# Changing the order of the first projections, the buffers of the RG-LRU stage and the share of projections beside it, in a one-core S5 and RG-LRU layer

## The chip, the core and the metric

The kernel runs on one core of one Trainium2 chip. The metric is the device time of one execution in microseconds; less is better. Three runs of the kernel before gave a median of 1853.79 us (1853.48 to 1860.08).

## What is computed

One layer of a diffusion backbone on x (2048 tokens, 1024 channels) behind a context of 256 tokens, all in f32. Both are normalised and modulated, projected to 4096 columns, run through two recurrent branches, gated, projected back and added to x.

```python
z = (rmsnorm(h, norm_g) * (1.0 + sc) + sh) @ w_in            # the same for the context
u_s5, g_s5, u_lru, g_lru = split(z)                          # 1024 columns each
# S5: 64 groups of 64 complex states, both directions, the context first
h_re, h_im = scan(abar, bbar @ u_s5);  y = gelu(c @ h + d * u_s5);  y = y * sigmoid(y @ w_glu + b_glu)
# RG-LRU: tokens in column-major order, both directions d
xc = depthwise_conv4(u_lru)
r, gi = sigmoid(xc @ w_a[d] + b_a[d]), sigmoid(xc @ w_x[d] + b_x[d])    # 16 heads of 64
a = exp(-8 * r * softplus(-lam));  h = scan(a, sqrt(1 - a * a) * gi * xc)
out = rmsnorm(x + gt * (concat(y_s5 * silu(g_s5), y_lru * silu(g_lru)) @ w_out), final_g)
```

## The kernel before, in words

Channels lie on the 128 partitions and tokens along a row. A **block** is 128 of the 1024 channels of one kind (`u_lru`, `g_lru`, `u_s5`, `g_s5`), so each kind has eight. A matmul in near-f32 is three matmuls on a high and a low part (`mm3`, lines 248 to 250), and weights are split into these parts by a cast on ScalarE (L240) and a subtraction on VectorE (L241).

`projections(half, kinds)` goes through the blocks of one half of the tokens. A block has a tile of 512 tokens for each of two quarters and, in the first half for `u` kinds, one of 256 context tokens ("c"). A **step** is one `yield` of it: the three matmuls of one of eight contraction parts, so eight steps make a tile. `merge(main, [side, rate])` advances a side generator by `rate` for each step of the main one; `islice(proj, n)` takes n steps. What is issued in which order is settled when the kernel is built: Tile's scheduler starts from the order of the program, and each engine then works strictly through its own list. Inside the RG-LRU loop TensorE's list is the program's own order (`manual_schedule`).

*First half.* `projections(0, ...)` runs with `prepare()` beside it at 0.1375: the S5 tables on VectorE (`s5_tables`, L625 to 627, with transposes L657 and lag matmuls L673 on TensorE), then the normalisation of quarters 2 and 3 (`xhat`) and the gate row. A `u_lru` tile is copied to `uc` (L314); when the block is complete, `conv` makes the four-tap convolution in `xcv` (L376 on ScalarE, three L379 on VectorE) and stores it to `XC` in DRAM (L381, POOL's queue), the context part first. `uc` and `xcv` have one buffer each.

*RG-LRU stage.* `lru()` handles eight blocks of both directions over 2304 tokens. For each direction five gate steps (L422: four 64x64 matmul tiles for `rr` and `gi`, into one buffer each of the PSUM pools `psG` and `psT`, which have two) are followed by sigmoids (L426). Then tanh (L467), `gi*xc` (L470), exp (L474), sqrt (L482), and `finish`: (a+1)*t (L432), L433, the scans (L437, L439), the sum of directions (L442), the product with the gate `GL` (L446) and the store `YL`. `finish` of a block runs as `prev` beside the gates of the next. The numbers that `lru` yields say how many projection steps of the second half TensorE does there: one behind each gate step, then 8, 8, 8 and 10: 44 for a block.

*S5 stage.* `s5_inputs` (L743, copies L746 to 750) fills `z0` and then `z1`, 32 groups each; `s5_scan` is 144 steps of three small VectorE instructions (L771 to 773) for each; `s5_outputs` (L804, L806) reads a finished scan. The rest of the projections, `out_lru` (matmuls `po`) and the scans are merged by rates. `glu` and `tail`, on TensorE alone, end the kernel.

Of the kernel before, what the change touches and what calls it, by code (L numbers as in the profile page):

```python
# [19 lines left out]
L = 2048  # L20
LC = 256
# [4 lines left out]
T = 16  # L26
# [14 lines left out]
def drain(gen):  # L41
    if gen is not None:
        for _ in gen:
            pass


class Block:
# [204 lines left out]
    def projections(self, half, kinds):  # L252
# [29 lines left out]
        both = [2 * half, 2 * half + 1]  # L282
        blocks = []
# [6 lines left out]
        if half == 0:  # L290
            blocks.remove(("g_lru", 0, both))
            blocks[:1] = [("u_lru", 0, ["c", 0]), ("g_lru", 0, [0]), ("u_lru", 0, [1]), ("g_lru", 0, [1])]
        raw, nxt = self.first if half == 0 else (load(0), None)
# [91 lines left out]
    def lru(self, lp, le):  # L385
# [16 lines left out]

        def load(b):

            xs = big("xs", 1, le)
            for e in range(2):
                o = b * P + 64 - e * 64
                nc.sync.dma_start(out=xs[e * 64:e * 64 + 64, :], in_=self.XC[o:o + 64, :])
            xc = big("xc", 1, le)
            nc.sync.dma_start(out=xc, in_=self.XC[rows(b), :])  # L410
            return xc, xs

# [16 lines left out]
        def finish(b, aa, gi, tt):  # L429

            for d in range(2):
                v.scalar_tensor_tensor(out=tt[d], in0=aa[d], scalar=1.0, in1=tt[d], op0=ALU.add, op1=ALU.mult)  # L432
                v.tensor_mul(out=gi[d], in0=gi[d], in1=tt[d])  # L433
                yield
                f = (lambda t, s: t[:, s]) if d == 0 else (lambda t, s: t[:, s][:, ::-1])
                init = tt[d][:, LC - 1:LC] if d == 0 else tt[d][:, 0:1]
                v.tensor_tensor_scan(out=f(tt[d], c_), data0=f(aa[d], c_), data1=f(gi[d], c_), initial=0.0,  # L437
                                     op0=ALU.mult, op1=ALU.add)
                v.tensor_tensor_scan(out=f(tt[d], x_), data0=f(aa[d], x_), data1=f(gi[d], x_), initial=init,  # L439
                                     op0=ALU.mult, op1=ALU.add)  # L440
                yield
            v.tensor_add(out=tt[1][:, x_], in0=tt[1][:, x_], in1=tt[0][:, x_])  # L442
            yo = big("rr", 3)[:, :L].rearrange("p (j q r) -> p j q r", j=T, q=4)
            g = big("gi", 3)[:, :L]
            nc.sync.dma_start(out=g, in_=self.GL[rows(b), :])
            v.tensor_mul(out=yo, in0=tt[1][:, x_].rearrange("p (q j r) -> p j q r", q=4, j=T),  # L446
                         in1=g.rearrange("p (q j r) -> p j q r", q=4, j=T))
# [4 lines left out]
        xcs = load(0)  # L452
        yield 28
        prev = iter(())
        for b in range(8):
            rr, gi, tt = [], [], []
            for d in range(2):
                rr.append(big("rr", 3))
                gi.append(big("gi", 3))
                for i, _ in enumerate(gates(b, d, gw, xcs, rr[d], gi[d])):  # L460
                    if i % 2 == 0:
                        next(prev, None)
                    yield 1
            drain(prev)
            for d in range(2):
                tt.append(big("tt", 3))
                th = nc.scalar.activation(out=tt[d], in_=rr[d], func=AF.Tanh,  # L467
                                          scale=self.c8h[:, d * 8 + b:d * 8 + b + 1])
            for d in range(2):
                v.tensor_mul(out=gi[d], in0=gi[d], in1=xcs[0])  # L470
            yield 8
            with self.tc.issue_after(th.ins):
# [567 lines left out]
    def build(self):  # L1040
        tc, nc = self.tc, self.nc
        with ExitStack() as es:
# [23 lines left out]
            with ExitStack() as eP:  # L1066
# [13 lines left out]
                with ExitStack() as eA, ExitStack() as eS:  # L1080
# [133 lines left out]
```

## Time and profile before

| | before |
|---|---|
| median of three runs | 1853.79 us |
| profiled execution, its own time | 1854.51 us |
| span of its trace | 1852.7 us |
| PE, DVE, ACT busy | 93%, 63%, 47% of the span |
| first projection matmul, first gate matmul | 54.7, 618.3 us |
| last gate matmul, first copy to `z0` | 943.9, 993.5 us |
| S5 scans, from step 2 to the last | 1061.7 to 1337.8 us |

The span goes from the first to the last instruction; the other 1.8 us lie around it. A busy PE is not PE at its peak, since overlapping matmuls are modelled. PE is TensorE, DVE VectorE, ACT ScalarE, POOL GpSimd; "<-" behind idle time names what ended it.

### The profile page before, as it was taken

What the parts mean: (1) busy time and instruction counts of PE and PEld (TensorE: products, weight loads), DVE (VectorE), ACT (ScalarE), POOL (GpSimd) and SP (SyncE); (2) the same over time, 40 slices, a digit from 0 to 9 for tenths busy, and PEclk for the clock granted to TensorE, in tenths of its full rate; (3) what the DMA queues carried; (4) which work ended last, traced back from release to release, by engine and by line L of the source; (5) the groups of instructions that cost most, each with busy time, mean ns of one, the idle gap of its engine ahead of it and who ended that gap; (6) DMA issues with size and microseconds to landing.
All of it is one profiled execution on the core that took longest, in us unless ns stands there. A gap on an engine that the chain in (4) does not pass through costs nothing.

```text
span 1852.7 us, 25971 instructions
## 1 busy us (share of the span) xinstructions
PE 1714.9 (93%) x9785; PEld 1372.4 (74%) x9785; DVE 1165.6 (63%) x2006; ACT 875.1 (47%) x1382; POOL 138.4 (7%) x268
## 2 busy tenths in 40 slices
PE   7887899999999899999998987869799999999997
PEld 2675778888887465666667876758698899998886
DVE  5789999974124287887774198999800056446663
ACT  3622332222562587786685877216355443222221
POOL 1112222211000000000000000000000000001111
PEclk9888999999999898999999999979899999999999
DMA  9675578876446555667777777228788766556563
GB/s 273 169 172 214 201 237 253 263 266 234 138 137 223 161 208 184 205 233 203 202 201 234 244 233 233 80 62 258 212 246 259 213 209 201 165 159 216 185 193 88
DMA packets 335470, 373.55 MB, mean 202 GB/s; under 512 B 124029, under 2 KB 274161, under 8 KB 323058
## 3 DMA queue, kind: packets, MB, share of 16 engines
q1 hardware_dynamic: 288304, 243.43, 45.8%
q0 software_dynamic: 20672, 94.91, 13.6%
q10 hardware_dynamic: 26370, 33.57, 5.2%
q8 instruction: 77, 1.26, 0.3%
q14 instruction: 47, 0.39, 0.1%
HBM read 233.49 MB, written 138.35 MB: 201 GB/s over the span
## 4 chain that ended last, share of the span: by engine, by line
PE 51%; issue 17%; DVE 16%; DMA 10%; ACT 4%; SPq 1%; POOL 1%; ACTq 0%; DVEq 0%; POOLq 0%
PE pp L248 7%; PE pp L249 7%; PE pp L250 7%; PE po L250 4%; PE po L248 4%; PE po L249 4%; DVE p L771 4%; PE pgl L250 3%; PE pgl L248 3%; PE pgl L249 3%; DVE z L772 3%; DVE z L773 3%; DMA YT<-y 2%; PE pw L743 2%; PE pg L422 1%
## 5 line engine op out<-in xcount | busy, mean ns | idle before, releaser
L248 PE MATMUL pp<-x,w 128*128 128x512 f32 x1024 | 422.9, 413 | 14.0 <-ACT uc L314 13.5
L250 PE MATMUL pp<-x,w 128*128 128x512 f32 x1024 | 407.3, 398 | 2.6 <-DVE w L241 2.6
L249 PE MATMUL pp<-x,w 128*128 128x512 f32 x1024 | 407.4, 398 | 0.0
L248 PEld LDWEIGHTS pp<-x,w 128*128 128x128 f32 x1024 | 194.9, 190 | 117.0 <-issue 65.6
L250 PEld LDWEIGHTS pp<-x,w 128*128 128x128 f32 x1024 | 195.0, 190 | 45.6 <-DVE w L241 3.4
L249 PEld LDWEIGHTS pp<-x,w 128*128 128x128 f32 x1024 | 195.5, 191 | 37.2 <-DVE x L213 1.0
L241 DVE TENSOR_TENSOR w<-wraw,w 128x1024 fp32r<-128x1024 f32 x66 | 80.5, 1220 | 163.0 <-ACT w L240 163.0
L240 ACT CAST w<-wraw 128x1024 fp32r<-128x1024 f32 x66 | 69.1, 1047 | 134.6 <-PE pp L250 101.6
L806 PE MATMUL py<-h,et 128*128 128x128 f32 x512 | 83.5, 288 | 33.3 <-ACT h L799 16.8
L250 PE MATMUL po<-x,w 128*128 128x512 f32 x256 | 101.9, 398 | 7.8 <-DVE w L241 7.8
L771 DVE TENSOR_TENSOR p<-z,A 128x128 f32<-128x128 f32 x288 | 104.0, 379 | 5.7
L248 PE MATMUL po<-x,w 128*128 128x512 f32 x256 | 104.4, 408 | 2.2 <-ACT x L836 1.6
L743 PE MATMUL pw<-u,wt 128*128 128x144 f32 x512 | 77.6, 300 | 26.1 <-DMA wt<-WD 18.2
L249 PE MATMUL po<-x,w 128*128 128x512 f32 x256 | 101.1, 395 | 0.2 <-DVE x L837 0.2
L422 PE MATMUL pg<-xc,gw 64*64 64x512 f32 (+1 forms) x320 | 92.2, 595 | 8.5 <-DMA GL<-ust 8.0
L248 PE MATMUL po<-ws,yh 128*128 128x512 f32 x256 | 99.6, 389 | 0.0
L249 PE MATMUL po<-ws,yh 128*128 128x512 f32 x256 | 99.6, 389 | 0.0
L250 PE MATMUL po<-ws,yl 128*128 128x512 f32 x256 | 99.6, 389 | 0.0
L743 PEld LDWEIGHTS pw<-u,wt 128*128 128x128 f32 x512 | 73.2, 200 | 34.4 <-issue 15.4
L806 PEld LDWEIGHTS py<-h,et 128*128 128x128 f32 x512 | 71.5, 202 | 36.0 <-ACT h L799 19.5
L422 PE MATMUL pg<-xs,gw 64*64 64x512 f32 (+1 forms) x320 | 91.0, 594 | 2.7 <-ACT gi L426 2.7
L379 DVE SCALAR_TENSOR_TENSOR xcv<-uc,vcol,xcv 128x256 f32<-128x256 f32 (+2 forms) x72 | 73.0, 1014 | 22.0 <-ACT xcv L376 21.3
(258 smaller groups left out, 3557.0 us busy)
## 6 DMA issues: line engine op xcount, KB each, us to landing
wraw<-in_w_in_dram SPq DMA_DIRECT2D x50, 512.0 KB
WS<-w POOLq DMA_DIRECT2D x24, 1024.0 KB, 7.0
w<-WS SPq DMA_DIRECT2D x24, 1024.0 KB
u<-ZU SPq DMA_DIRECT2D x64, 288.0 KB
ED<-E POOLq DMA_DIRECT2D x16, 1024.0 KB, 5.6
WD<-Wt POOLq DMA_DIRECT2D x32, 512.0 KB, 4.2
wt<-WD SPq DMA_DIRECT2D x32, 512.0 KB
et<-ED SPq DMA_DIRECT2D x32, 512.0 KB
```

The lines of the kernel that those rows point to most:

```text
L240: copy(out=w[:, 0], in_=raw)
L241: self.nc.vector.tensor_sub(out=w[:, 1], in0=raw, in1=w[:, 0])
L248: nc.tensor.matmul(ps, lhsT=whi(k), rhs=xhi(k), start=(k == 0), stop=False)
L249: nc.tensor.matmul(ps, lhsT=whi(k), rhs=xlo(k), start=False, stop=False)
L250: nc.tensor.matmul(ps, lhsT=wlo(k), rhs=xhi(k), start=False, stop=(k == KT - 1))
L379: nc.vector.scalar_tensor_tensor(out=xc, in0=u[:, o + k:o + k + N], scalar=cw[:, k * 8 + b:k * 8 + b + 1], in1=xc, op0=ALU.mult, op1=ALU.add)
L422: nc.tensor.matmul(pss[w][e * 64:e * 64 + 64, :n], lhsT=gw[ws, d, e, :], rhs=xcs[(w + e) % 2][ws, o:o + n], start=True, stop=True, tile_po ...
L743: nc.tensor.matmul(pw[:, c, :], lhsT=w[:, gi, kt, c, :], rhs=u[:, kt, :], start=(kt == 0), stop=(kt == 1))
L771: v.tensor_mul(out=p, in0=cur.unsqueeze(1).to_broadcast([P, 2, 2, 32]), in1=self.A16[:, :, :, gs])
L772: v.tensor_add(out=nxt, in0=nxt, in1=p[:, 0])
L773: v.tensor_add(out=nxt, in0=nxt, in1=p[:, 1, ::-1])
L806: nc.tensor.matmul(o, lhsT=ms(e[:, i, gi]), rhs=h[:, i, :], start=False, stop=(i == 1))
```

## The change

Four things are changed. (1) In the first half `u_lru` and `g_lru` of block 0 stay in front; then come `u_s5`, `g_s5`, `g_lru` and, last, the other seven `u_lru`. (2) In the RG-LRU stage `gi` gets four buffers and `tt` two; the scans write into `gi`, the gate `GL` is loaded into the spent `rr` and the product goes into the spent `gi`, so `rr` and `gi` no longer take extra buffers. The loads of the next block's `xs`, `gw` and `xc` are issued right behind the gates. (3) Gate steps come in pairs, with one projection step behind each pair and 8, 8 and 16 later: 37 for a block instead of 44. (4) Behind the stage 32 projection steps are taken beside `s5_inputs` of `z0` at 1.0 instead of 56 at 0.57, and the rates of the next merge are lower, as more steps are left.

```diff
         if half == 0:
-            blocks.remove(("g_lru", 0, both))
-            blocks[:1] = [("u_lru", 0, ["c", 0]), ("g_lru", 0, [0]), ("u_lru", 0, [1]), ("g_lru", 0, [1])]
+            blocks = [("u_lru", 0, ["c", 0]), ("g_lru", 0, [0]), ("u_lru", 0, [1]), ("g_lru", 0, [1])] + [
+                bl for bl in blocks if bl[:2] not in (("u_lru", 0), ("g_lru", 0))]
...
-                init = tt[d][:, LC - 1:LC] if d == 0 else tt[d][:, 0:1]
-                v.tensor_tensor_scan(out=f(tt[d], c_), data0=f(aa[d], c_), data1=f(gi[d], c_), initial=0.0,
+                init = gi[d][:, LC - 1:LC] if d == 0 else gi[d][:, 0:1]
+                v.tensor_tensor_scan(out=f(gi[d], c_), data0=f(aa[d], c_), data1=f(gi[d], c_), initial=0.0,
...
-            v.tensor_add(out=tt[1][:, x_], in0=tt[1][:, x_], in1=tt[0][:, x_])
-            yo = big("rr", 3)[:, :L].rearrange("p (j q r) -> p j q r", j=T, q=4)
-            g = big("gi", 3)[:, :L]
+            g = aa[1][:, :L]
             nc.sync.dma_start(out=g, in_=self.GL[rows(b), :])
+            v.tensor_add(out=gi[1][:, x_], in0=gi[1][:, x_], in1=gi[0][:, x_])
+            yield
+            yo = gi[0][:, :L].rearrange("p (j q r) -> p j q r", j=T, q=4)
...
                 rr.append(big("rr", 3))
-                gi.append(big("gi", 3))
-                for i, _ in enumerate(gates(b, d, gw, xcs, rr[d], gi[d])):
-                    if i % 2 == 0:
+                gi.append(big("gi", 4))
+                for i, _ in enumerate(gates(b, d, gw, (xc, xs), rr[d], gi[d])):
+                    if (d * 5 + i) % 2 == 1:
+                        yield 1
                         next(prev, None)
-                    yield 1
-            drain(prev)
+                v.tensor_mul(out=gi[d], in0=gi[d], in1=xc)
+            if b < 7:
+                xs, gw, xc = load_xs(b + 1), weights(b + 1), load_xc(b + 1)
             for d in range(2):
-                tt.append(big("tt", 3))
+                tt.append(big("tt", 2))
...
-            if b < 7:
-                gw, xcs = weights(b + 1), load(b + 1)
-            yield 8
...
-            yield 10
+            yield 16
...
-                    merge(self.projections(0, (("u_lru",), ("u_s5",), ("g_lru",), ("g_s5",))), [side, 0.1375])
+                    merge(self.projections(0, (("u_s5",), ("g_s5",), ("g_lru",), ("u_lru",))), [side, 0.1375])
...
-                merge(islice(proj, 56), [sin[0], 0.57])
+                merge(islice(proj, 32), [sin[0], 1.0])
...
-                merge(proj, [sin[1], 0.5], [scans[0], 1.5], [load, 0.17])
+                merge(proj, [sin[1], 0.25], [scans[0], 0.9], [load, 0.1])
```

The built orders show where this lands. On VectorE, in the first half, this stood in a stretch of `u_lru` blocks before; xcv is the convolution, E, W and ot are the S5 tables:

```order
L379 SCALAR_TENSOR_TENSOR xcv<-uc,vcol_372,xcv 128x256
L626 TENSOR_TENSOR ot<-PI,WE 128x512
L379 SCALAR_TENSOR_TENSOR xcv<-uc,vcol_372,xcv 128x256
L627 TENSOR_TENSOR W<-W,ot 128x512
L379 SCALAR_TENSOR_TENSOR xcv<-uc,vcol_372,xcv 128x256
L626 TENSOR_TENSOR ot<-PI,WE 128x512
```

And this stands in the changed kernel where the second `u_lru` block is convolved (line numbers are three higher there from `lru` on):

```order
L630 TENSOR_TENSOR W<-W,ot 128x512
L241 TENSOR_TENSOR w<-wraw,w 128x1024
L688 SCALAR_TENSOR_TENSOR kk<-dmask,dcol,psk 128x16
L690 TENSOR_TENSOR kk<-kk,psk 128x16
L379 SCALAR_TENSOR_TENSOR xcv<-uc,vcol_372,xcv 128x256 x3
L241 TENSOR_TENSOR w<-wraw,w 128x1024
L383 COPY halo<-uc 128x3
L379 SCALAR_TENSOR_TENSOR xcv<-uc,vcol_372,xcv 128x1022 x3
```

All E and W rows now stand ahead of the seven moved convolutions, which are no longer mixed with them.

On TensorE, in the gates of an RG-LRU block before (pg is a gate tile, pp a projection):

```order
L422 MATMUL pg<-xc,gw 64x512
L422 MATMUL pg<-xs,gw 64x512 x2
L422 MATMUL pg<-xc,gw 64x512
L248 MATMUL pp<-x_4498,w 128x512
L249 MATMUL pp<-x_4498,w 128x512
L250 MATMUL pp<-x_4498,w 128x512
```

And now:

```order
L425 MATMUL pg<-xc,gw 64x512
L425 MATMUL pg<-xs,gw 64x512 x2
L425 MATMUL pg<-xc,gw 64x512 x2
L425 MATMUL pg<-xs,gw 64x512 x2
L425 MATMUL pg<-xc,gw 64x512
L248 MATMUL pp<-x_4286,w 128x512
L249 MATMUL pp<-x_4286,w 128x512
L250 MATMUL pp<-x_4286,w 128x512
```

Two gate steps, which fill all four buffers of `psG` and `psT`, now stand together.

On VectorE, where the second S5 scan joins the first before (`z_7430` is the first scan, `z_7431` the second):

```order
L771 TENSOR_TENSOR p<-z_7430,A_318 128x128
L771 TENSOR_TENSOR p<-z_7431,A_318 128x128
L772 TENSOR_TENSOR z_7430<-z_7430,p 128x64
L772 TENSOR_TENSOR z_7431<-z_7431,p 128x64
L773 TENSOR_TENSOR z_7430<-z_7430,p 128x64
L773 TENSOR_TENSOR z_7431<-z_7431,p 128x64
```

And the changed kernel, shortly ahead of that place (`z_7201` is the first scan):

```order
L776 TENSOR_TENSOR z_7201<-z_7201,p 128x64
L774 TENSOR_TENSOR p<-z_7201,A_318 128x128
L241 TENSOR_TENSOR w<-wraw,w 128x1024
L775 TENSOR_TENSOR z_7201<-z_7201,p 128x64
L776 TENSOR_TENSOR z_7201<-z_7201,p 128x64
L774 TENSOR_TENSOR p<-z_7201,A_318 128x128
```

Before, the first scan does 82 of its 144 steps by itself, the second 89, and 61 and 55 are mixed as shown; now 109 and 113 stand by themselves and 34 and 31 are mixed. From step 2 of the first scan to the end of the second, VectorE's list had 14 weight subtractions L241 before and has 21 now.

## Rows read from the trace of the kernel before

**Rows 1.** Windows: us, then busy us (instructions) by engine, PEclk, DMA share, GB/s

```profile
113.00:261.00 148.00, 127.50 (x779) 100.89 (x779) 136.66 (x185) 44.86 (x79) 35.23 (x68) 0.91 0.56 200
618.00:944.00 326.00, 322.56 (x1592) 193.49 (x1593) 241.00 (x117) 250.50 (x283) 7.46 (x18) 0.97 0.61 190
...
1062.00:1158.00 96.00, 76.71 (x425) 66.31 (x423) 86.85 (x259) 70.56 (x158) 0.00 (x0) 0.95 0.74 234
1158.00:1240.00 82.00, 63.29 (x264) 50.86 (x264) 81.24 (x348) 12.47 (x18) 3.19 (x6) 0.91 0.22 71
1240.00:1338.00 98.00, 82.03 (x542) 75.58 (x542) 88.76 (x288) 52.57 (x79) 1.60 (x3) 0.92 0.70 213
1338.00:1491.00 153.00, 146.65 (x947) 133.00 (x948) 16.39 (x17) 79.40 (x122) 3.72 (x7) 0.98 0.82 249
717.00:728.00 11.00, 10.86 (x33) 3.83 (x37) 10.93 (x6) 7.31 (x11) 0.14 (x2) 0.54 0.41 145
994.00:1030.00 36.00, 33.57 (x184) 29.07 (x184) 2.63 (x3) 32.02 (x75) 0.00 (x0) 0.91 0.86 266
```

**Rows 2.** Timeline of ACT, one u_lru block of the first half: start, duration, instruction

```profile
208.44 1.35 ACT L314 COPY uc<-pp 128x256 f32<-128x256 f32 x3 [3.16 <-DVE xcv L379]
215.44 0.60 ACT L376 ACTIVATE xcv<-uc,vcol 128x256 f32<-128x256 f32 x1 [5.64 <-DMA XC<-xcv]
...
221.15 1.24 ACT L376 ACTIVATE xcv<-uc,vcol 128x1022 f32<-128x1022 f32 x1
...
229.31 1.35 ACT L314 COPY uc<-pp 128x256 f32<-128x256 f32 x3 [4.74 <-DVE xcv L379]
```

**Rows 3.** Timeline of POOL, the stores of the same block

```profile
208.63 0.54 POOL L381 DMA_DIRECT2D XC<-xcv  x1 [0.65 <-DVE xcv L379]
...
218.91 0.56 POOL L381 DMA_DIRECT2D XC<-xcv  x1 [0.90 <-DVE xcv L379]
```

**Rows 4.** Groups by line and shape: busy us, mean ns, idle before

```profile
L241 DVE TENSOR_TENSOR w<-wraw,w 128x1024 fp32r<-128x1024 f32 x66 | 80.5, 1220 | 163.0 <-ACT w L240 163.0
...
L439 DVE TENSOR_TENSOR_SCAN tt<-rr,tt,gi 128x2048 f32<-128x2048 f32 x16 | 71.5, 4477 | 0.2
...
L426 ACT ACTIVATE rr<-pg,vcol 128x512 f32<-128x512 f32 x64 | 44.2, 690 | 38.4 <-PE pg L422 37.4 <-DVE tt L437 0.9
...
L432 DVE SCALAR_TENSOR_TENSOR tt<-rr,tt 128x2304 f32<-128x2304 f32 x16 | 40.7, 2554 | 38.7 <-ACT tt L482 38.7
...
L467 ACT ACTIVATE tt<-rr,c8h 128x2304 f32<-128x2304 f32 x16 | 35.5, 2221 | 0.5
...
L379 DVE SCALAR_TENSOR_TENSOR xcv<-uc,vcol,xcv 128x1022 f32<-128x1022 f32 x24 | 30.7, 1278 | 0.8 <-ACT xcv L376 0.8
...
L379 DVE SCALAR_TENSOR_TENSOR xcv<-uc,vcol,xcv 128x256 f32<-128x256 f32 x24 | 11.5, 480 | 6.0 <-ACT xcv L376 5.9
```

**Rows 5.** Timeline of PE: gate steps, then the projections up to the next block's gates

```profile
843.08 0.64 PE L422 MATMUL pg<-xc,gw 64*64 64x512 f32 x1
...
844.10 0.50 PE L248 MATMUL pp<-x,w 128*128 128x512 f32 x1
...
844.99 0.64 PE L422 MATMUL pg<-xc,gw 64*64 64x512 f32 x1
...
858.34 0.50 PE L248 MATMUL pp<-x,w 128*128 128x512 f32 x1
...
882.37 0.43 PE L422 MATMUL pg<-xc,gw 64*64 64x256 f32 x1
```

**Rows 6.** Timeline of DVE: S5 scan steps, alone and with both scans mixed

```profile
1290.59 0.38 DVE L771 TENSOR_TENSOR p<-z,A 128x128 f32<-128x128 f32 x1
...
1291.63 0.38 DVE L771 TENSOR_TENSOR p<-z,A 128x128 f32<-128x128 f32 x1
...
1186.32 0.67 DVE L771 TENSOR_TENSOR p<-z,A 128x128 f32<-128x128 f32 x2
...
1187.61 0.67 DVE L771 TENSOR_TENSOR p<-z,A 128x128 f32<-128x128 f32 x2
```

More of the change, by code (lines that the diff above doesn't have):

```diff
@@ L401, in weights, with load_xs @@
             return gw
-        def load(b):
+        def load_xs(b):
             xs = big("xs", 1, le)
@@ L408, in load, with load_xc @@
                 nc.sync.dma_start(out=xs[e * 64:e * 64 + 64, :], in_=self.XC[o:o + 64, :])
+            return xs
+        def load_xc(b):
             xc = big("xc", 1, le)
             nc.sync.dma_start(out=xc, in_=self.XC[rows(b), :])
-            return xc, xs
+            return xc
         def gates(b, d, gw, xcs, rr, gi):
@@ L435, in finish @@
                 f = (lambda t, s: t[:, s]) if d == 0 else (lambda t, s: t[:, s][:, ::-1])
-                init = tt[d][:, LC - 1:LC] if d == 0 else tt[d][:, 0:1]
-                v.tensor_tensor_scan(out=f(tt[d], c_), data0=f(aa[d], c_), data1=f(gi[d], c_), initial=0.0,
+                init = gi[d][:, LC - 1:LC] if d == 0 else gi[d][:, 0:1]
+                v.tensor_tensor_scan(out=f(gi[d], c_), data0=f(aa[d], c_), data1=f(gi[d], c_), initial=0.0,
                                      op0=ALU.mult, op1=ALU.add)
-                v.tensor_tensor_scan(out=f(tt[d], x_), data0=f(aa[d], x_), data1=f(gi[d], x_), initial=init,
+                v.tensor_tensor_scan(out=f(gi[d], x_), data0=f(aa[d], x_), data1=f(gi[d], x_), initial=init,
                                      op0=ALU.mult, op1=ALU.add)
                 yield
-            v.tensor_add(out=tt[1][:, x_], in0=tt[1][:, x_], in1=tt[0][:, x_])
-            yo = big("rr", 3)[:, :L].rearrange("p (j q r) -> p j q r", j=T, q=4)
-            g = big("gi", 3)[:, :L]
+            g = aa[1][:, :L]
             nc.sync.dma_start(out=g, in_=self.GL[rows(b), :])
-            v.tensor_mul(out=yo, in0=tt[1][:, x_].rearrange("p (q j r) -> p j q r", q=4, j=T),
+            v.tensor_add(out=gi[1][:, x_], in0=gi[1][:, x_], in1=gi[0][:, x_])
+            yield
+            yo = gi[0][:, :L].rearrange("p (j q r) -> p j q r", j=T, q=4)
+            v.tensor_mul(out=yo, in0=gi[1][:, x_].rearrange("p (q j r) -> p j q r", q=4, j=T),
                          in1=g.rearrange("p (q j r) -> p j q r", q=4, j=T))
@@ L451, in lru @@
         gw = weights(0)
-        xcs = load(0)
+        xs, xc = load_xs(0), load_xc(0)
         yield 28
@@ L458, in lru @@
                 rr.append(big("rr", 3))
-                gi.append(big("gi", 3))
-                for i, _ in enumerate(gates(b, d, gw, xcs, rr[d], gi[d])):
-                    if i % 2 == 0:
+                gi.append(big("gi", 4))
+                for i, _ in enumerate(gates(b, d, gw, (xc, xs), rr[d], gi[d])):
+                    if (d * 5 + i) % 2 == 1:
+                        yield 1
                         next(prev, None)
-                    yield 1
-            drain(prev)
+                v.tensor_mul(out=gi[d], in0=gi[d], in1=xc)
+            if b < 7:
+                xs, gw, xc = load_xs(b + 1), weights(b + 1), load_xc(b + 1)
             for d in range(2):
-                tt.append(big("tt", 3))
+                tt.append(big("tt", 2))
                 th = nc.scalar.activation(out=tt[d], in_=rr[d], func=AF.Tanh,
                                           scale=self.c8h[:, d * 8 + b:d * 8 + b + 1])
-            for d in range(2):
-                v.tensor_mul(out=gi[d], in0=gi[d], in1=xcs[0])
             yield 8
+            drain(prev)
             with self.tc.issue_after(th.ins):
```

## The prediction, as it was put on record

> **What bounds the kernel now.** I read the table of engines first: PE is busy for 93% of the span, DVE for 63%, ACT for 47%. A kernel in that state can gain from a new order only the time in which PE is idle or runs at a lower clock, so the next view was the windows, cut where the program changes its stage [rows 1]. They show three kinds of stage. In the RG-LRU stage PE is full (322.6 us of 326, clock 0.97): nothing is idle there, and a shorter stage means that its projections are done elsewhere. In the first 148 us with `u_lru` blocks PE is busy for 127.5 us and the clock is 0.91, so 20.5 us are idle and the low clock takes up to 0.09 x 148 = 13 us more. In the S5 scans (1062 to 1338 us, 276 us) VectorE is busy 86.85, 81.24 and 88.76 us of 96, 82 and 98, 93% together, while PE is busy for 222 us and idle for 54: VectorE's chain of scan steps sets the end, PE has room. Behind the last scan PE is full again (146.65 of 153).
>
> So the change can win up to 34 us in the first half, and whatever projection steps it moves out of the full RG-LRU stage into the scans' 54 idle us, as long as they don't lengthen the scans.
>
> **Part A, `u_lru` last in the first half: -20 us.** Seven blocks are affected. The timeline of ACT for one of them shows a period of 229.31 - 208.44 = 20.9 us, with 5.64 us for the store of the context part before `xcv` may be written again [rows 2]. PE needs less: a matmul of 512 tokens takes (882.37 - 858.34) / 105 = 0.229 us at 35 steps of three matmuls, 0.687 us a step, in the tight stretch behind the gates [rows 5]; a `u_lru` block has 48 such matmuls and 24 of 256 tokens, for which I take half, an estimate: 11.0 + 2.7 = 13.7 us. The chain through the single buffers `uc` and `xcv` is what the period consists of. Without the table rows that VectorE now mixes into it, it has: copies and the landing of the earlier store, 215.44 - 208.63 = 6.8 us from the store's issue [rows 2, 3]; the short convolution, 0.60 + 3 x 0.48; its store until ScalarE's next write, 221.15 - 218.91 = 2.2; the long one, 1.24 + 3 x 1.28 [rows 2 to 4]. That is 6.8 + 2.0 + 2.2 + 5.1 = 16.1, with 0.5 for hand-overs 16.6 us: 4.3 less, and 30 us for seven blocks. Of this I give back 10: the transposes and lag matmuls of the tables lay in these gaps of PE, and now take its time in the full stretch of the `s5` blocks. Ends: -30, and 0 if the chain stays at 20.9 because something else (the normalisation of quarters 2 and 3, which uses ScalarE and VectorE too) lies beside the blocks at their new place.
>
> **Part B, the RG-LRU stage: -28 us.** A block now has 35 steps in a tight row, 24.0 us, and 10 gate steps with a projection step each, 10 x (844.99 - 843.08) = 19.1 less the shorter ones of 256 tokens, about 18.7 [rows 5]: 42.7 us. The changed block has 32 steps in the tight row, 21.9 us, and five pairs. For PE a pair is two gate steps (844.10 - 843.08 = 1.02 each), 0.2 between kinds (0.89 behind a gate step less 0.69) and one step, 2.9 us: 14.6, or 13.6 with the shorter ones. But a pair fills all four PSUM buffers, and the next waits for four sigmoids of 0.69 on ScalarE [rows 4]: 20 of them take about 13 us and a tanh of 2.2 stands between the directions, so I take 16. The shared buffer rule gives another end: sqrt, then L432 and L433 (2.55 each) and the scans with 4.48 and some 0.7 are 10.3 us of VectorE before `gi` and `rr` come free [rows 4]; this lay and lies beside the tight row, 1.3 us of it I leave on the path. The sum is 39.2, 3.5 less for each of eight blocks: -28. Ends: -45 (gates at PE's floor, no chain) and 0 (each pair waits so long for its sigmoids that 42.7 stays). This is work moved, not saved: 8 x 7 = 56 steps of 0.687 are 38 us of PE that leave the stage, and 10 of them are lost again in the pairs.
>
> **Part C, entry to the first gates: +3 us.** These need `XC` of block 0, stored long before; but the last block's convolution (0.6 + 1.4 + 1.2 + 3.8 = 7.1 us [rows 2, 4]) now stands ahead of the first sigmoids in ScalarE's and VectorE's lists. I take half of it; ends 0 and one chain, 16.6.
>
> **Part D, `s5_inputs` of `z0`: -6 us.** 24 fewer steps are 16.4 us of PE. But in the 36 us of this stretch ACT is busy for 32.0 and the DMA engines are at 0.86 with 266 GB/s [rows 1]: the stretch can't become shorter than the copies, so 4 to 6 us are all I count. Ends -16.4 and 0.
>
> **Part E, the S5 scans: +28 us.** The 56 + 24 steps come back here: 55 us of PE, about as much as the 54 it is idle, and more weight subtractions for VectorE. The lowered rates also let the first scan run alone for longer. A step that stands alone takes 1.04 us, since each of its three instructions waits for the one before; in a mixed pair of steps they cover each other, 1.29 for two, 0.645 each [rows 6]. By the orders, lone steps rise from 171 to 222 and mixed ones fall from 116 to 65: 51 x (1.04 - 0.645) = 20; seven subtractions more cost 7 x 1.22 = 8.5 [rows 4]. VectorE is 93% busy here, so nothing hides them. Ends: 20 (subtractions slip into the gaps between the instructions of lone steps) and 36 (PE, full now, delays copies to `z1`).
>
> The Trainium skill (VectorE: DVE Perf Modes, section "The DRAIN you can't avoid") says that a VectorE instruction starts when the pipe behind the one before has emptied, and that taking the semaphores out of a row of eight copies gained nothing; by that a lone and a mixed step would cost the same, part E would be 8.5 and the time 1821. The trace of this kernel differs, 1.04 against 0.645 [rows 6], and the page grants that an instruction that is not held starts earlier; I keep the trace, and give such an outcome 0.03, inside the first rival's chance.
>
> **Part F, behind the scans: +10 us.** In the built order 444 of the 768 `po` matmuls stand ahead of the second outputs, 480 before: 36 x 0.229 = 8.2 us come to a stretch where PE is full [rows 1]. Ends 8 and 16.
>
> The sum: -20 - 28 + 3 - 6 + 28 + 10 = -13, from the profiled execution's 1854.5 to 1841.5; that execution is 0.7 above the median of the runs, so I say 1841. As a check by PE's idle time: 20.5 + 54 idle us before; A uses 10 to 20 of them, the scans about 20.
>
> **The rivals.** (1) *It runs smoothly:* A at its full 30, gates at PE's floor (21.9 + 13.6 + 1.3 = 36.8, 41 us in seven blocks), scans +20, the end +8: -30 - 41 + 3 - 6 + 20 + 8 = -46, 1808 us. For it: PE is full in this stage, so ScalarE (250.5 of 326) has room [rows 1]. Against it: that room is not where the pairs need it.
>
> (2) *The moved steps come back in full:* the convolution chain stays at 20.9 us at its new place, so A is 0, and the rest as summed: +7, 1861 us, no change. For it: the 5.64 us wait is for a DMA [rows 2], which no new order of VectorE shortens. Against it: 4.3 us of the period have no other owner than table work.
>
> (3) *Slower, the clock falls in the pairs:* PE now stands still between pairs, where a projection step behind each gate step kept it busy. The trace has such a case: from 717 to 728 us in the same stage the granted clock is 0.54, near the lower of its two levels of 1.2 and 2.4 GHz, which costs 11 x 0.46 = 5.1 us [rows 1]. Once in each of eight blocks that is 41 us: -13 + 41 = +28, 1882 us after the 0.7. It decides from the fifth block on: (13 + 9.3) / 5.1 = 4.4. Against it: it happened rarely in a stage at 0.97 mean, with these gate steps in it.
>
> The Trainium skill (TensorE: Matmul & The Clock Gate, section "A second HAM failure mode: psum-queue depth-cycling") describes this: cycling through PSUM buffers leaves short idle times between groups of matmuls, and the clock swings between its levels. The stretch at 0.54 [rows 1] is in line with it, and so far the trace bears it out for one block of eight.
>
> (4) *The change does not act:* Tile's scheduler places the rows as before. The orders shown speak against it.
>
> **How the numbers follow.** The summed case gets 0.45, with a range of its own of 1826 to 1855 (A and B each half-way to either end). The smooth one gets 0.20, the one that comes back in full 0.18, the clock 0.14, and 0.03 for no action or something not thought of. About 0.5%, 9.3 us, is what a measurement of this kernel can tell from no change: below 1844.5 is faster, above 1863.1 slower. Faster: 0.34 of the summed case and all of the smooth one, 0.54. Same: the rest of the summed case, 0.11, and 0.16 of the second rival, 0.27. Slower: the clock, 0.02 of the second rival and the last 0.03, 0.19. The range reaches from the smooth case (half of it lies below 1804) to 1866, beyond the second rival, and leaves the clock out.
>
> **What would show it.** A: the period of the copies to `uc` in the last seven blocks of the first half, 16 to 18 us if right, 21 if the second rival holds. B: 38 to 40 us from one block's first gates to the next's; the idle time ahead of the gate matmuls ended by ACT on `pg`; and a granted clock under 0.9 in that stage if the clock decides. C and D: first gate matmul, and copies to `z0` until step 2. E: about 304 us from step 2 to the last, with lone steps still at 1.04; if lone steps hide the subtractions, nearer 296. F: 8 to 16 us more from the last scan step to the end. I am wrong most easily in E, if `xc` and the gate's load, moved in SP's queue, or the full PE bring a wait into the scans that the trace of before doesn't have.

## The result and the profile after

The changed kernel took 1867.86 us in the median of 20 runs (1857.61 to 1878.07), the kernel before 1855.87 (1851.68 to 1865.89). The ratio is 1.0059, with a 95% interval of 1.0042 to 1.0077: 8 to 14 us slower, where 1841 was predicted and 1866 was the upper end of the range. The profiled execution took 1859.89 us, 8 less than the median. A second profile of the same kernel, taken later, is of an execution of 1869.67, and stands beside it:

| stage, us | before | after | after, second profile | predicted change |
|---|---|---|---|---|
| up to the first projection | 54.7 | 56.0 | 57.1 | 0 |
| from there to the first gates | 563.6 | 557.4 | 561.5 | A + C: -17 |
| first to last gate | 325.6 | 295.1 | 299.3 | B and D: -34 |
| last gate to step 2 of the first scan | 117.8 | 105.2 | 107.3 | in B and D |
| step 2 to the last scan step | 276.1 | 314.0 | 314.8 | E: +28 |
| from there to the end | 514.9 | 530.4 | 527.8 | F: +10 |

The windows of the changed kernel, cut at its own stages (us; then busy us by engine with instructions; PEclk, DMA share, GB/s), answer to [rows 1]:

```profile
98.00:438.00 340.00, 329.07 (x2023) 262.55 (x2023) 279.19 (x354) 92.83 (x168) 64.70 (x109) 0.99 0.73 228
438.00:556.00 118.00, 111.55 (x611) 92.52 (x609) 48.11 (x67) 63.07 (x99) 15.05 (x38) 0.97 0.55 184
556.00:613.00 57.00, 42.37 (x177) 33.08 (x175) 27.05 (x27) 12.39 (x20) 1.94 (x6) 0.91 0.66 221
613.00:909.00 296.00, 278.30 (x1431) 173.42 (x1432) 237.12 (x115) 245.27 (x276) 6.93 (x17) 0.97 0.59 196
...
1014.00:1144.00 130.00, 109.39 (x540) 91.81 (x539) 117.40 (x346) 69.97 (x145) 0.00 (x0) 0.91 0.59 182
1144.00:1328.00 184.00, 149.14 (x838) 132.25 (x837) 162.38 (x554) 75.76 (x122) 3.72 (x7) 0.91 0.56 175
...
1328.00:1493.00 165.00, 158.82 (x996) 141.75 (x996) 18.84 (x19) 82.35 (x127) 4.25 (x8) 1.00 0.78 233
```

The moved `u_lru` blocks lie in 438 to 556. Behind them TensorE has a hole, 14.6 us idle in 57. In the scans (1014 to 1328) it is idle for 55.5 us, as before (54), although 36 us more of its work stands there (258.5 us busy against 222). TensorE's idle time in the scans, which was to take the moved steps, wasn't used up; the stretch grew by about as much as the work that was put there.

Where the new time lies is in the waits of PE in the scans, 1015 to 1328 us (engine, line, for what: us in total, times, longest):

```profile
PE py L809 <- DMA et<-ED: 24.2, 4, 8.7
PE pw L746 <- ACT gst L336: 11.6, 1, 11.6
PE pw L746 <- DMA wt<-WD: 6.6, 1, 6.6
PE pp L250 <- DVE w L241: 5.4, 5, 2.0
```

And in the kernel before, 1062 to 1338 us:

```profile
PE pw L743 <- DMA wt<-WD: 15.3, 7, 3.9
PE py L806 <- ACT h L799: 15.3, 1, 15.3
PE po L250 <- DVE w L241: 7.8, 3, 3.1
PE py L806 <- DMA et<-ED: 7.4, 4, 5.6
```

Here `wt` and `et` are tables loaded from DRAM for the matmuls of `s5_inputs` (`pw`) and `s5_outputs` (`py`), and `gst` is the buffer of a `g_s5` tile's activation. The second row of the changed kernel is new: in the kernel before, this wait is 1.6 us, ahead of the scans. In the second profile it is 12.1. The timelines show who holds whom, first PE (start, duration, instruction, idle before):

```profile
1059.50 0.39 PE L250 MATMUL pp<-x,w 128*128 128x512 f32 x1
1071.49 2.29 PE L746 MATMUL pw<-u,wt 128*128 128x144 f32 x8 [11.61 <-ACT gst L336]
```

ACT, the same stretch:

```profile
1059.92 0.62 ACT L839 CAST x<-wfraw 128x512 fp32r<-128x512 f32 x1 [7.87 <-PE pp L250]
1060.45 1.04 ACT L240 CAST w<-wraw 128x1024 fp32r<-128x1024 f32 x1
1070.84 0.60 ACT L336 ACTIVATE gst<-pp 128x512 f32<-128x512 f32 x1 [9.35 <-DVE x L840]
```

DVE, the same stretch:

```profile
1059.66 0.38 DVE L774 TENSOR_TENSOR p<-z,A 128x128 f32<-128x128 f32 x1
...
1069.83 0.37 DVE L774 TENSOR_TENSOR p<-z,A 128x128 f32<-128x128 f32 x1
1070.13 0.68 DVE L840 TENSOR_TENSOR x<-wfraw,x 128x512 fp32r<-128x512 f32 x1
```

Read from the bottom: `whalf` loads pieces of `w_out` into the two buffers `st2`, which the activations of the projections (`gst`) use too. The cast of its first piece (L839) waits for the last projection of quarter 2, whose tile the target `x2` reuses. Its subtraction (L840) has nine scan steps ahead of it in VectorE's list. Until it has run, `gst` has no buffer, PSUM isn't emptied, and PE waits. Before, quarter 2 was projected by the time the load began; with 78 steps moved behind (56 and 24, less 2 that the last block's longer `finish` takes), it isn't.

### The profile page after: what moved, and what is told of

Its sections match the earlier page's. It is cut to its first block, busy times and chain, and to the rows that moved or that the text cites. A ratio compares the mean times of both kernels' runs of the same rounds, so it can differ in the third digit from the quotient of the medians.

```text
span 1858.1 us, 25994 instructions
## 1 busy us (share of the span) xinstructions
PE 1704.8 (92%) x9785; PEld 1379.3 (74%) x9785; DVE 1187.0 (64%) x2006; ACT 866.4 (47%) x1378; POOL 137.7 (7%) x268
## 5 line engine op out<-in xcount | busy, mean ns | idle before, releaser
L241 DVE TENSOR_TENSOR w<-wraw,w 128x1024 fp32r<-128x1024 f32 x66 | 80.5, 1220 | 143.7 <-ACT w L240 135.2
L240 ACT CAST w<-wraw 128x1024 fp32r<-128x1024 f32 x66 | 69.2, 1048 | 152.4 <-PE pp L250 107.7
L746 PE MATMUL pw<-u,wt 128*128 128x144 f32 x512 | 79.5, 306 | 31.5 <-ACT gst L336 11.6
L379 DVE SCALAR_TENSOR_TENSOR xcv<-uc,vcol,xcv 128x256 f32<-128x256 f32 (+2 forms) x72 | 73.1, 1015 | 55.3 <-ACT xcv L376 53.3
L425 PE MATMUL pg<-xc,gw 64*64 64x512 f32 (+1 forms) x320 | 88.9, 582 | 12.6 <-issue 11.7
```

The costliest lines, as they stand in the source:

```text
L240: copy(out=w[:, 0], in_=raw)
L241: self.nc.vector.tensor_sub(out=w[:, 1], in0=raw, in1=w[:, 0])
L379: nc.vector.scalar_tensor_tensor(out=xc, in0=u[:, o + k:o + k + N], scalar=cw[:, k * 8 + b:k * 8 + b + 1], in1=xc, op0=ALU.mult, op1=ALU.add)
L425: nc.tensor.matmul(pss[w][e * 64:e * 64 + 64, :n], lhsT=gw[ws, d, e, :], rhs=xcs[(w + e) % 2][ws, o:o + n], start=True, stop=True, tile_po ...
L746: nc.tensor.matmul(pw[:, c, :], lhsT=w[:, gi, kt, c, :], rhs=u[:, kt, :], start=(kt == 0), stop=(kt == 1))
```

## The experiments

Ratios are to the kernel before, run on the same chip in the same series, with 95% intervals. By this measure the changed kernel is 1.0059.

**1. The new order alone** (`e1`): the kernel before with `projections`' order and `merge` call of the change.

> Only the new order of the first half, everything else as before. Theory (the order wins a little, since TensorE's idle time in it mostly comes back ahead of the first gates): first gates 5 to 6 us earlier, nothing else moves, about 1850 us against 1856 of before. Rival (the order itself is what costs the changed kernel its 12 us): 1862 to 1868.

Measured: 1849.93 us, 0.9963 (0.9945 to 0.998). The order wins some 7 us.

**2. The change without the new order** (`e2`).

> The changed kernel with the old order of the first half. Theory: it loses the 5 to 6 us of the order, about 1873 us against 1868 of the changed kernel, with scans of about 312 us as there. Rival (the order costs): 1856 or less.

1873.96 us, 1.0094 (1.0071 to 1.0116). The order isn't the loss. PE waits 13.2 us for `gst` here too.

**3. The change with the old number of steps** (`e3`).

```diff
-            yield 16
+            yield 23
-                merge(islice(proj, 32), [sin[0], 1.0])
+                merge(islice(proj, 56), [sin[0], 0.57])
-                merge(proj, [sin[1], 0.25], [scans[0], 0.9], [load, 0.1])
+                merge(proj, [sin[1], 0.5], [scans[0], 1.5], [load, 0.17])
```

> The changed kernel with 44 projection steps for a block (8, 8, 23 behind the five of the pairs), and 56 steps at 0.57 and the old rates behind the stage. Theory (steps moved out of the RG-LRU stage cost more in the scans than they free): period of a block about 45 us, scans back to 275 us, the sum 1859 us, 9 less than the changed kernel. Rival (moved steps are neutral, the shared buffers and pairs cost): 1868 or more.

1855.06 us, 0.9999 (0.9978 to 1.002). The whole loss of the changed kernel against the one before is in the moved steps and what goes with them.

**4. A slower first scan** (`e4`).

```diff
-                merge(proj, [sin[1], 0.25], [scans[0], 0.9], [load, 0.1])
+                merge(proj, [sin[1], 0.28], [scans[0], 0.5], [load, 0.1])
```

> The changed kernel with the first scan at 0.5 of a step for each projection step instead of 0.9, and the copies to z1 at 0.28 instead of 0.25, so that by the order 126 scan steps stand alone and 162 are mixed, instead of 221 and 67. Theory (lone steps lengthen the scans): 95 x 0.395 = 38 us of VectorE's time go, of which TensorE's work lets 25 to 35 through: scans 275 to 285 us, 1835 to 1843 us in all. Rival (what VectorE waits for is ScalarE's copies and the loads, not the lone steps): within 5 us of 1868.

1875.23 us, 1.0108 (1.0086 to 1.0131): slower, where 25 to 35 us of gain were expected. The wait for `gst` stays (12.6 us), and from 1017.5 to 1338.7 us VectorE stands still 37 us for the casts of weights that its list has next (L241 behind L240). The scan steps that were put back there follow behind the projections. The end has a row of its own, the waits of PE behind the last outputs:

```profile
PE pgl L248 <- ACT yh L968: 12.8, 1, 12.8
```

`glu` must wait for the outputs to be stored, loaded again and split (`yh`). The changed kernel has 108 `po` matmuls left to do between its last `py` and `glu`; here none is left, they were spent earlier.

**5. `z1` first** (`e5`).

```diff
-                merge(proj, [sin[1], 0.25], [scans[0], 0.9], [load, 0.1])
+                merge(islice(proj, 40), [sin[1], 0.8], [scans[0], 1.2], [load, 0.1])
+                drain(sin[1])
+                merge(proj, [scans[0], 0.6], [scans[1], 0.6], [load, 0.1])
```

> The changed kernel with the copies to z1 first: they go at 0.8 beside the next 40 projection steps (the first scan at 1.2), and both scans at 0.6 beside the remaining 72; by the order 100 scan steps stand alone and 188 are mixed, instead of 221 and 67. Theory (behind the last projection the end is set by VectorE's chain, and it is long because the second scan can't start until z1 is full at 1159 us): z1 full before 1090 us, scans 245 to 265 us instead of 312, the sum 1815 to 1835 us. Rival (TensorE has no room for moved steps anywhere in this stretch): within 8 us of 1868.

1864.2 us, 1.004 (1.002 to 1.006). The scans took 284 instead of 314 us in its profile, but the stretch from their end to `glu` 190 instead of 165: a shorter scan only moved TensorE's work behind it. VectorE's chain was not what set the end of the kernel.

**6. More `po` beside the scans** (`e6`): the side's rates 0.28 and 0.2 become 0.45 and 0.4.

> The changed kernel with more matmuls po beside the scans: the rates 0.28 and 0.2 of the side become 0.45 and 0.4, so that 288 instead of 216 po matmuls stand ahead of the first outputs. Theory (TensorE is idle in the scans because its list has too little there that doesn't wait for VectorE): scans stay at 312 us and 15 to 25 us of po go from behind them, 1843 to 1855 us. Rival (the idle time is made of waits that no further po can fill, since the list is in order): within 5 us of 1868 or above.

1881.22 us, 1.0125 (1.0101 to 1.015). `glu` waits 12.9 us as in `e4`, with no `po` left ahead of it here either, and the scans take no less.

**7. More steps ahead of the first gates** (`e7`): `yield 28` becomes `yield 40`.

> The changed kernel with 40 instead of 28 projection steps ahead of the first gates. Theory (TensorE is idle there for 11.7 us while xs and xc of block 0 are loaded, and only room of this kind can take projections for nothing): first gates not later, 12 x 0.687 = 8 us less work behind, 1858 to 1862 us. Rival (the loads start later by as much, since their store follows a projection step): 1868.

1868.4 us, 1.0062 (1.0039 to 1.0085). The hole was filled (4.6 us of wait instead of 11.7), but the gates took 7 to 11 us longer than in the two profiles of the changed kernel. Their window has the lower clock, the third value from the end (0.97 in the changed kernel):

```profile
620.00:926.00 306.00, 284.59 (x1429) 175.12 (x1428) 233.93 (x113) 242.09 (x271) 6.96 (x17) 0.94 0.57 186
```

From the first gate on, TensorE waits 17.8 us for sigmoids here (10.5 in the changed kernel). The lower level comes in five blocks, from 713, 754, 798, 842 and 883 us on, each time for 3 to 7 us and next to such a wait (once more, from 699.5 us, behind a wait for weights).

**8. The shared buffers without pairs** (`e8`): a step behind every gate step, 44 steps, rates as in `e3`.

> The new order and the shared buffers, with a projection step behind every gate step again, 44 steps for a block and the old rates behind the stage. It differs by its gate steps alone from the run with pairs and 44 steps, which took 1855 us, and by the buffers alone from the run with the order alone, 1850 us. Theory (the pairs cost the 5 us, TensorE waits for the sigmoids between them): 1850 us, period of a block 43.8 us. Rival (the shared buffers cost them): 1855 us, period about 44.

1854.94 us, 0.9986 (0.9971 to 1.0001), the same as with pairs. The pairs cost nothing that can be measured; whether the buffers cost the 4 us to `e1` lies within the intervals.

**9. The load of `w_out` later** (`e9`).

```diff
-                merge(proj, [sin[1], 0.25], [scans[0], 0.9], [load, 0.1])
+                merge(islice(proj, 56), [sin[1], 0.25], [scans[0], 0.9])
+                merge(proj, [sin[1], 0.25], [scans[0], 0.9], [load, 0.17])
```

> The changed kernel with the loads and splits of the first half of w_out begun 56 projection steps later (at 0.17 from there on); nothing else differs. In the profile of the changed kernel TensorE stands still for 11.6 us at 1060 us, since the activation of a g_s5 tile waits for one of the two buffers st2; a piece of w_out holds it, whose target x2 is free only behind the last projection of quarter 2 and whose subtraction stands behind scan steps on VectorE. Theory (this new wait and the clock behind it are the loss): no wait at that place, 1850 to 1856 us against 1868, about as with 44 steps for a block (1855). Rival (78 steps moved into the scans cost more there than they free, as I expected in the first runs): 1863 or more.

1862.97 us, 1.0021 (1.0006 to 1.0036): two thirds of the loss are gone. The wait for `gst` is gone, but waits for the subtractions L241, which stand behind scan steps as well, have risen:

```profile
PE pp L250 <- DVE w L241: 13.7, 8, 2.3
```

**10. `z1` first and the load later** (`e10`): the edits of `e5` and `e9` (the load at 0.17 behind 56 steps).

> Both edits: z1 filled first (which alone gave 1864 us) and the loads of w_out 56 steps later. Theory (the wait for st2): it had 3.9 us of this wait at the activation and 6.3 us of subtractions late; 1852 to 1860 us. Rival (mixing the scans gains by itself once the wait is gone): below 1850.

1854.53 us, 0.9979 (0.9962 to 0.9997), 0.6% less than `e5`, from the load's place alone.

**11. The new order with more `po`** (`e11`): `e1` with the side at 0.42 instead of 0.28.

> The new order of the first half alone (1850 us), with the side of the mixed scans at 0.42 instead of 0.28, so that 408 instead of 384 po matmuls stand ahead of the first outputs. Theory: TensorE waits 13.8 us there for the end of the first scan, and 24 more matmuls fill 5.5 us of it: 1843 to 1847 us. Rival (work put into the scans is only given back, as with more po in the changed kernel): 1850 or more.

1864.93 us, 1.004 (1.0026 to 1.0055), 0.8% worse than `e1`. The 13.8 us ahead of the first outputs went, and came back in the waits of PE behind the scans:

```profile
PE pgl L248 <- ACT yh L965: 12.1, 1, 12.1
PE py L806 <- DMA et<-ED: 5.7, 3, 2.5
```

In `e1` there is no wait for `yh` at this place, and 9.0 us of waits for `et`. In all, TensorE is idle there for 20 us of 162, against 7 of 150 in `e1`.

**12. Buffers of their own for `w_out`** (`e12`): nothing but

```diff
-            raw = (rp or self.stp).tile([P, 512], F32, tag="st2", bufs=2, name="wfraw")
+            raw = self.gt[:, k % 2 * 512:k % 2 * 512 + 512] if tag == "x2" else (rp or self.stp).tile(
+                [P, 512], F32, tag="st2", bufs=2, name="wfraw")
```

> The changed kernel, with the pieces of the first half of w_out in two buffers of their own (in the row that later holds the gate) instead of the two st2 that the activations of the projections use too. All rates as in the changed kernel. Theory (the wait is for the shared buffer): no wait at 1060 us, 1850 to 1858 us. Rival (ScalarE's list stands still behind the cast that waits for x2, whatever the buffer; or the wait is not the loss): 1863 or more.

1859.64 us, 1.0007 (0.9996 to 1.0018). One shared buffer is 0.5% of the time, about all by which the change was slower. Waits of PE in the scans:

```profile
PE pp L250 <- DVE w L241: 13.9, 8, 2.7
...
PE pw L746 <- ACT gst L336: 1.5, 1, 1.5
```

**13. A faster preparation with the new order** (`e13`): `e1` with the rate 0.155 instead of 0.1375.

> The new order of the first half alone (1850 us), with the preparation beside it at 0.155 instead of 0.1375. There TensorE waits for the normalisation of quarters 2 and 3 (6.3 and 2.3 us) and for the gate row (4.1 us), which now lie between the last blocks of the half. Theory (the gain of the order is given back because the preparation ends as late as the projections do): these waits go, first gates 5 to 9 us earlier, 1841 to 1846 us. Rival (they only stand where other waits would stand: the tables then press on VectorE earlier): 1848 or more.

1851.75 us, 0.9968 (0.9947 to 0.9989), the same as `e1`; the theory falls. The 12.3 us that TensorE is idle ahead of the first gates in `e1` are gone, but the first gates don't come earlier (621.9 us, 617.2 in `e1`; 564.5 and 559.5 behind the first projection). The normalisation and the gate row are waited for as before, the tables more (PE, 56 to 625 us):

```profile
PE psw L657 <- DVE W L627: 8.6, 6, 2.0
...
PE pst L205 <- ACT xrow L196: 5.4, 1, 5.4
PE psg L172 <- DVE gacc L167: 5.3, 1, 5.3
```

**14. Own buffers and the first scan at 0.7** (`e14`): `e12` with `[scans[0], 0.7]`.

> The changed kernel with buffers of their own for the pieces of w_out (which alone gave 1859.6 us), and the first scan at 0.7 instead of 0.9 of a step for each projection step; 179 scan steps alone and 109 mixed. In the profile with own buffers TensorE waits 13.9 us for subtractions L241 that stand behind scan steps in VectorE's list. Theory (these waits are the rest of the loss against the run with 44 steps, 1855): 3 to 6 us of them and of lone steps gained, 1853 to 1857 us. Rival (the moved steps themselves are the rest): 1858 or more.

1850.29 us, 0.9962 (0.9942 to 0.9981), as fast as `e1`. But the waits for L241 are 13.5 us as in `e12`, so the theory had the wrong owner. Its windows, up to the last projection and from there to the last scan step:

```profile
1023.00:1143.00 120.00, 105.63 (x537) 88.25 (x536) 100.21 (x286) 69.28 (x145) 0.00 (x0) 0.97 0.67 202
1143.00:1330.00 187.00, 156.14 (x842) 136.37 (x841) 169.37 (x613) 72.56 (x117) 4.26 (x8) 0.91 0.52 162
```

`e12` has 123 and 184 us there, 307 in both: 42 fewer lone steps did not shorten the scans. But TensorE is busy for 156.1 us of the second window, 148.6 in `e12`, as more mixed steps bring more `po` matmuls by the side's rate (420 in the scans, 372 in `e12`); and from the last scan step to `glu` it takes 160 us instead of 169. That is the gain, as the profiles show it.

**15. The changed kernel again** (`e15`).

> The changed kernel once more, for a second profile: the first profiled execution took 1860 us, 8 less than the median of its runs. Theory: about 1868 us, with the same wait of some 12 us at the activation of a g_s5 tile, and more time at the lower clock. Rival: the extra time lies in a stage that the first profile shows undisturbed.

1869.67 us. The wait for `gst` is 12.1 us and the scans as long as in the first profile; of the additional 10 us 4.1 lie ahead of the first gates, 4.2 in the gates, 2.1 behind them, 0.8 in the scans and 1.1 in a later start, while the end is 2.6 shorter. So the rival holds. What the theory said of the clock holds too: 0.962 on average instead of 0.965, about 6 us of 1868.

**16. Own buffers and `z1` first** (`e16`): `e12` with the `merge` lines of `e5`.

> The changed kernel with buffers of their own for the pieces of w_out (alone 1859.6 us) and z1 filled first, both scans at 0.6 beside the last 72 projection steps (alone 1864 us, with the loads 56 steps later 1854.5). 100 scan steps alone, 188 mixed. Theory (with the buffer's wait gone, fewer lone steps shorten the stretch, as with the scan at 0.7, 1850.3): 1846 to 1851 us. Rival (TensorE's work and its other waits set the end; a scan that ends earlier only lengthens what is behind it): 1852 to 1856 us.

1851.94 us, 0.9973 (0.9952 to 0.9994). It can't be told from `e14` or `e1`: 79 fewer lone steps than in `e14` gain nothing that can be measured.

No version is clearly ahead of the new order alone. `e1`, `e13`, `e14` and `e16` beat the kernel before by 0.3% to 0.4%, `e10` by 0.2%.

## Why the prediction was wrong

Between the predicted -13 and the measured +12 lie 25 us. By the table, with the mean of the profiles for A, A with C holds 13 of them, E 10 and F 3 to 5; B and D gave more than was said.

**Part A failed in its size.** -20 was predicted for the order, -17 with C; over the 14 profiles with the new order, the old rate of the preparation and 28 steps ahead of the gates, the first gate starts at 612.8 to 618.6 us, mean 616.1, against 618.3 in the profile before and 622.4 in `e2`, so about -4. By whole kernels the order is worth some 7 us (`e1`; the changed kernel against `e2`). The mechanism was right as far as it went: the chain of a block has become shorter, as the timeline of ACT shows for a moved block, where the copies of [rows 2] answer:

```profile
475.64 0.86 ACT L314 COPY uc<-pp 128x256 f32<-128x256 f32 x2 [3.03 <-DVE xcv L379]
480.11 0.60 ACT L376 ACTIVATE xcv<-uc,vcol 128x256 f32<-128x256 f32 x1 [3.61 <-DMA XC<-xcv]
...
484.79 1.24 ACT L376 ACTIVATE xcv<-uc,vcol 128x1022 f32<-128x1022 f32 x1 [1.62 <-DMA XC<-xcv]
...
490.10 0.86 ACT L314 COPY uc<-pp 128x256 f32<-128x256 f32 x2 [1.42 <-DVE rs L193]
```

The wait for the store is 3.61 us instead of 5.64. The seven blocks need 118 us, the window 438 to 556, 16.9 each. That this is near the predicted 16.6 is luck: TensorE is busy for 111.55 of the 118, with transposes and table matmuls between the blocks, and waits nowhere there for `uc`, so its own list sets this time and not the chain. What failed is the step from the chain to the stage: 4.3 us saved in each of seven blocks were counted as 30 us less for TensorE, of which 10 were given back. But all that TensorE waited for the chain before were the 13.5 us of the first row here (113 to 271 us; the other two are from 560 to 619):

```profile
PE pp L248 <- ACT uc L314: 13.5, 4, 6.0
...
PE pg L422 <- DMA GL<-ust: 8.0, 1, 8.0
PE psg L172 <- DVE gacc L167: 0.7, 1, 0.7
```

These 13.5 us went, and as much came elsewhere. What must end is TensorE's list for the whole half, and its idle time moved: from 113 to 271 us it is 9.4 us instead of 20.5 (148.65 busy of 158; 137.5 before), but from 438 us to the first gates 21 (6.4 + 14.6), where 9 were idle before. In all, from the first projection to the first gates, it is idle for 33.9 us before and 33.5 after (36.6 in the second profile). The waits of PE from 438 to 614 us name it:

```profile
PE pg L425 <- issue: 11.7, 1, 11.7
PE pst L205 <- ACT xrow L196: 5.8, 2, 5.3
PE psg L172 <- DVE gacc L167: 3.3, 1, 3.3
```

The normalisation of quarters 2 and 3, named in the prediction as what would bring A to 0, now meets the `u_lru` blocks; `e13` shows that it isn't mended by an earlier preparation.

**Part C's number was right, its reason not.** The gap ahead of the gates, 8.0 us before, is 11.7, so +3 fits. But no sigmoid waits for a convolution, as the last row shows, where ACT waits for PE; and `XC` of block 0 isn't stored long before, since its last part is, in both kernels, the first work of the second half. In the changed kernel:

```profile
592.58 0.19 ACT L362 COPY uc<-halo 128x3 f32<-128x3 f32 x1 [16.51 <-DMA GT<-gt]
...
602.38 1.12 SPq L408 DMA_DIRECT2D xs<-XC  x2
...
613.43 0.66 PE L425 MATMUL pg<-xc,gw 64*64 64x256 f32 x1 [11.67 <-issue]
...
614.67 0.47 ACT L429 ACTIVATE rr<-pg,vcol 128x256 f32<-128x256 f32 x1 [6.64 <-PE pg L425]
```

By the profile the copy for that part waits for the store of the gate row (`GT`), the last of the preparation; the convolution and its store (599.36, landed 602.37) follow, and the loads of `xs` and `xc` are issued behind them. In all 14 profiles the first gates come 22 to 23 us behind the issue of the `GT` store. In `e13` that store comes 29 us earlier than in `e1` and the gap is gone, but TensorE's other waits keep the first gates where they were.

**Parts B and D were right, and a little small:** -43 and -37 us in the two profiles against -34. The gates hold -30 and -26 of it (-28 predicted for B), the way from them to step 2 -13 and -10 (-6 for D, too small). The period from one block's gates to the next's is 40.0 us in the mean (613.4 to 893.5 in seven blocks), 39.2 predicted; before it was 43.8, where the prediction summed up 42.7. The pairs run at the floor that the prediction worked out (2.9 us) and didn't choose, as PE's timeline shows:

```profile
695.05 0.64 PE L425 MATMUL pg<-xc,gw 64*64 64x512 f32 x1
...
696.92 0.50 PE L248 MATMUL pp<-x,w 128*128 128x512 f32 x1
...
697.82 0.64 PE L425 MATMUL pg<-xc,gw 64*64 64x512 f32 x1
```

A pair and its step take 2.77 us. What keeps the mean at 40 is single events: the fifth period is 47.3 us, with 5.1 for weights from `WS` and a stretch at the lower clock (807 to 814 us). That this stage's gain is work moved was said, and holds.

**Part E failed in its premise.** +28 was said, +38 measured. The reasoning by lone steps was sound: they take 1.04 us as before, and a mixed pair 1.29 (DVE):

```profile
1168.06 0.67 DVE L774 TENSOR_TENSOR p<-z,A 128x128 f32<-128x128 f32 x2
...
1169.35 0.67 DVE L774 TENSOR_TENSOR p<-z,A 128x128 f32<-128x128 f32 x2
```

The 10 us that were missed are waits in VectorE's list, 11.6 us against 1.7. In the changed kernel, 1015 to 1328 us:

```profile
DVE x L840 <- ACT x L839: 6.6, 4, 4.3
DVE z L775 <- ACT z L750: 5.0, 1, 5.0
```

And in the kernel before, 1063 to 1338 us:

```profile
DVE x L837 <- ACT x L836: 1.7, 3, 0.8
```

The first belongs to the shared buffers, as the wait for `gst` does, and the prediction had not found it: it counted what the moved steps do to VectorE's chain, and not which buffers the steps now hold while others want them. `e12` takes away the sharing alone: the wait for the casts is 0.3 us, the scans take 307 us instead of 314, and the kernel gains 0.5%. The second is the second scan's wait for the last copies to `z1`. It is 4.3 us in `e12` too; the prediction had it at its upper end of 36 ("PE, full now, delays copies") and left it out of the 28.

The premise, that VectorE's chain sets the end and TensorE's 54 idle us take the moved steps, fell: TensorE is idle for 55.5 us as before, `e5` shortens the scans by 30 us and gains 0.2% in all, `e14` has 42 fewer lone steps than `e12` and scans as long, and `e16`, with scans of 279 us, is no faster than `e14`. So, as far as these show, TensorE's ordered list sets the end of the kernel. Its idle time there is made of waits for `et`, `wt`, `gst` and weights, and matmuls that stand elsewhere in the list don't fill them. Where in the list the `po` matmuls stand then matters: `e4`, `e6` and `e11` lose with so many of them beside the scans that none is left ahead of `glu`, and `e14` gains 0.45% over `e12` with more of them there and some left. That this is the cause in `e14` and `e4`, whose edits change the scans too, is argued and not shown. How much each wait for `et` owes to the moved steps (24 us in the scans, 7.4 before, when TensorE waited 15.3 for the end of the first scan at its first output) stays open; no run took it away.

**Part F was +10 with 16 as its end;** 15.5 and 12.9 were measured, with TensorE full (158.8 of 165). The 36 `po` matmuls were counted ahead of the second outputs; behind the last scan step lie 84 more than before (396, 312 before).

**The rivals.** The second (moved steps come back in full, 1861) was nearest, though its reason, an unchanged chain of 20.9 us, is wrong: TensorE's wait for the chain went, and others came. The third (the clock falls in the pairs) did not come in the changed kernel: 0.97 in the gates, as before. It is real all the same, as `e7` shows with 0.94 and the same pairs, only begun later: there the pairs wait longer for their sigmoids, 17.8 us, and the clock falls in five blocks. What makes them wait longer wasn't settled. The Trainium skill (TensorE: Matmul & The Clock Gate, section "A second HAM failure mode: psum-queue depth-cycling") describes a clock that swings when cycling through PSUM buffers leaves short idle times; here pairs alone don't bring it. On the Trainium skill's other rule (VectorE: DVE Perf Modes, section "The DRAIN you can't avoid"), that the next instruction starts when the pipe has emptied, the trace of the changed kernel differs as that of the one before did: 1.04 for a lone step, 0.645 for a mixed one.

**Two sums of the prediction don't come out.** The end of -45 for part B is not what its terms give (42.7 - 21.9 - 13.6 is 7.2 a block, 58 for eight). And A and B each half-way to their ends give 1827 to 1865 us, not 1826 to 1855, so the chance given to "faster" was too high for the prediction's own terms.

## What to carry to other kernels

Work moved out of a stage in which the bounding engine is full cost its full time where it went. To be free it would have to stand in the list at the very place of a wait there, so name the waits one by one; no run here shows that done. When steps are moved past a load, look up which buffers they share with it and what must end before its target is free: one shared pair of staging buffers cost 10 us here (`e12`). Before pricing a shorter chain, read what the bounding engine waits for it: 13.5 us here, and not seven times 4.3. Work behind a store and load round trip may be its cover; taking it forward brought a wait of 12 to 13 us in three experiments.

## What was not expected of the hardware

The clock fell in the new wait: TensorE was idle from 1059.9 to 1071.5 us, its granted clock went to the lower level at 1063.4 and stayed there until 1080.5, 9 us behind the wait's end; the window 1014 to 1144 has 0.91, and 0.96 to 0.97 stand there in `e12` and `e14`, where the wait is gone. Nine us of work at half the clock are at most 4.5 us, by estimate. Yet the kernel gained less than the wait's length without it (`e12`, some 10 us), since other waits rose. And the same kernel spread over 20 us in 20 runs (1857.61 to 1878.07), the kernel before over 14, so that one profiled execution was 8 us off its median. The granted clock goes along with it: 0.965 in the two fastest of the 20, 0.959 to 0.962 in the six slowest.
